# One 2048-column addition per load for the conditioning vectors, in three 8 KB slots, with six weight slots and eight units kept back at the end

## The chip, the cores and the metric

The kernel runs on one core of a Trainium2 chip. The metric is the device time of one launch in microseconds (us). Engines: TensorE (PE) multiplies, its weight loads are PEld; VectorE (DVE) and ScalarE (ACT) work on tiles; GpSimd (POOL) and SyncE (SP) issue transfers. The profile's line numbers are those of the kernel before.

## What is computed

A trunk of two layers on 256 tokens of width 2048, all in float32. Both layers are conditioned by a vector c; the first mixes tokens with a forgetting attention (FoX), the second with a sliding-window attention (SWA), and each is followed by a gated feed-forward block with a short convolution.

```python
c_act = silu(c)
for i in range(2):
    mod = c_act @ ada_w[i] + ada_b[i]            # 2048 x 12288
    sh1, sc1, g1, sh2, sc2, g2 = split(mod, 6)
    h = x * (1 + sc1) + sh1
    y = fox_attention(h, ...) if i == 0 else swa_attention(h, ...)
    x = layer_norm(alpha * x + (1 + g1) * y, ln_mix_g[i], ln_mix_b[i])
    h = x * (1 + sc2) + sh2
    y = conv_ffn(h, ffn_w_up[i], ffn_conv_w[i], ffn_conv_b[i], ffn_w_down[i])
    x = layer_norm(alpha * x + (1 + g2) * y, ln_ffn_g[i], ln_ffn_b[i])
```

## The kernel before

**Weights.** Every product runs through units of 512 KB of weights (256 rows by 512 columns), 728 in all. `stream` (L260) loads a unit into a slot `w` of the pool `wp` (10 slots of 4 KB per partition), ScalarE rounds it to `wh` (L268), and VectorE forms the rest `wl = w - wh` (L279); both lie in the pool `hl`, four pairs. TensorE then makes three products (high by high, high by low, low by high): 24 matmuls of 256 columns, or 12 of 512, per unit. A list `work` holds the units and the steps between them; `settle(2)` (L225) keeps the residuals two units ahead of the matmuls. All loads of `w`, `wa`, `wo` and `ln` are issued by SyncE in program order, each as soon as its slot is free.

**Conditioning vectors.** `mod` isn't computed on TensorE. `ada_vector` (L373) loads `ada_w` in blocks of 128 rows by 1024 columns into slots of the same `wp` pool (tile `wa`) and adds them, each scaled per partition by one column of silu(c), into the accumulator `acc` on VectorE (L395, L397). These operations are pinned, so they keep their program order among the other pinned operations. After each unit `ada_tick` (L469) adds a rate to a debt, and takes one step of `ada_vector` for each whole unit of debt; the rates are written out in the code (1.6 in the FoX projections, 1.3 in its output projection, 0.64 in the first feed-forward block). `ada_need` takes steps until a vector is there. Vectors with an index 2 or 5 are gates: they start from a bias row and are then spread over all partitions, the others are summed by TensorE.

**Opening.** The first two vectors of layer 0 are worked out at once, in five stages of column pairs, from tiles `wo` (L563) of the same pool, partly by additions on VectorE (L574, L576, into `oacc`), partly by products on TensorE (`cps`).

**Other buffers.** `gtile` (L60) gives a tile of 2 KB from the pool `gp` of 30: the FoX partial sums (`part`), the values `v` (L838), `qh`, `ql`, `kh`, `kl`, the gated activations `gT`. `hpad` (`hH`, L480) holds the modulated input in its high and low half, 32 KB per partition.

**Layer norm.** The gains and offsets come as rows, spread over the partitions by `ln_rows` (L659) into four `wp` slots of 1024 columns (tile `ln`), and are used by pinned operations on VectorE (L677, L678, and L1180, L1181 at the end).

**The end.** `x_mm_end` (L298) keeps the last units of the last product back: their matmuls for the first 128 tokens (t0) run at once, those for the other 128 (t1) after all of t0 are done, so that VectorE can finish t0 (`residual` L629, layer norm L1180/L1181, and the output's transfer) meanwhile. Two units are kept in layer 0, four in layer 1.

Of the kernel before, what the change touches and what calls it, by code (L numbers as in the profile page):

```python
# [10 lines left out]
F32 = mybir.dt.float32  # L11
# [30 lines left out]
def hybrid_trunk(ctx: ExitStack, tc: tile.TileContext, a: dict, out: bass.AP):  # L42
# [13 lines left out]
    def wtile(name="w"):  # L56
        return wp.tile([P, 2, WB], F32, tag="w", name=name)

# [201 lines left out]
    def stream(wsrc, row0, col, ks, use):  # L260

        for kc in ks[::2]:
# [3 lines left out]
            h = hl.tile([P, 2, WB], F32R, tag="wh", name="wh")  # L266
            l = hl.tile([P, 2, WB], F32R, tag="wl", name="wl")
# [54 lines left out]

    def x_stationary(wsrc, col, k0, nk, stat, end=0):

        ps = x_banks()
        use = x_mm_end(ps, stat, nk, end) if end else lambda kc, h, l: x_mm(ps, kc, h, l, stat, nk - 1)
        stream(wsrc, k0, col, list(range(nk)), use)
        return ps
# [44 lines left out]
    def ada_vector(l, v):  # L373
# [14 lines left out]
        for k in range(KC):  # L388
            for c in range(0, D, D // 2):
                w = wtile("wa").rearrange("p a f -> p (a f)")  # L390
                pin(nc.sync.dma_start(w, a["ada_w"][l, k * P:(k + 1) * P, v * D + c:v * D + c + D // 2]), False)
                for o in range(0, D // 2, step_):
                    ac, wo = part(c + o, step_), w[:, o:o + step_]
                    if k == 0 and not row:
                        pin(nc.vector.tensor_scalar_mul(ac, wo, cact[:, 0:1]), True)  # L395
                    else:
                        pin(nc.vector.scalar_tensor_tensor(ac, wo, (cactp if row else cact)[:, k:k + 1], ac,  # L397
                                                           op0=ALU.mult, op1=ALU.add), True)
                yield
# [61 lines left out]
    def ada_step():  # L461
        if ada["gen"] is None:
            if not ada_list or ada.get("held"):
                return
            ada["gen"] = ada_vector(*ada_list.pop(0))
        if next(ada["gen"], ada) is ada:
            ada["gen"] = None

    def ada_tick():  # L469
# [65 lines left out]
    def opening(plan, proj, prep):  # L535
# [21 lines left out]
        def sums(s_, c0, CB, acc, ps):  # L557
            QK = 512 // CB
            pe = onpe[s_]
            for kq in range(0, KC, QK):  # L560
                w = wp.tile([P, QK, 2, CB], F32, tag="w", name="wo")
# [647 lines left out]
```

## Time and profile before

| | us |
|---|---|
| median of 3 runs | 2213.51 (2211.17 to 2214.28) |
| profiled execution | 2215.89 |
| its span, first to last instruction | 2214.0 |
| TensorE busy | 2164.3 |
| VectorE busy | 1792.8 |
| ScalarE busy | 1159.6 |
| mean granted TensorE clock | 0.992 |

The busy times are those of the profiled execution, whose span is 1.9 us shorter than its device time. A row of groups names line, engine, operation, the tiles it writes and reads, partitions by elements and count, then busy us and mean ns of one, then the idle time before it and what ended it. In a timeline the first number is the start in us from the span's start, the second the duration, and `x2` two such operations in a row. A row of the DMA issues gives count, KB of one, and the median us from issue to landing.

### The profile page before, as it was taken

What the parts mean: (1) busy time and instruction counts of PE and PEld (TensorE: products, weight loads), DVE (VectorE), ACT (ScalarE), POOL (GpSimd) and SP (SyncE); (2) the same over time, 40 slices, a digit from 0 to 9 for tenths busy, and PEclk for the clock granted to TensorE, in tenths of its full rate; (3) what the DMA queues carried; (4) which work ended last, traced back from release to release, by engine and by line L of the source; (5) the groups of instructions that cost most, each with busy time, mean ns of one, the idle gap of its engine ahead of it and who ended that gap; (6) DMA issues with size and microseconds to landing.
All of it is one profiled execution on the core that took longest, in us unless ns stands there. A gap on an engine that the chain in (4) does not pass through costs nothing. (4 is left out here: it accounts for less than half of the span.)

```text
span 2214.0 us, 38357 instructions
## 1 busy us (share of the span) xinstructions
PE 2164.3 (98%) x14915; PEld 1976.7 (89%) x14915; DVE 1792.8 (81%) x2459; ACT 1159.6 (52%) x1841; POOL 19.0 (1%) x48
## 2 busy tenths in 40 slices
PE   6999999999999999999999999999999999999997
PEld 5999888789999988999987877789999988999986
DVE  6879998989978979799798888789888655666756
ACT  3435656465565543655644677555555533555532
POOL 0000000000000000000000000000000000000000
PEclk9999999999999999999999999999999999999999
DMA  9999998979978989899797676678888566666663
GB/s 334 368 352 366 351 352 298 327 257 323 349 234 300 322 312 385 260 311 322 251 354 290 201 240 206 208 257 295 281 264 270 187 194 195 192 195 195 191 195 108
DMA packets 274246, 602.98 MB, mean 272 GB/s; under 512 B 21062, under 2 KB 29960, under 8 KB 273552
## 3 DMA queue, kind: packets, MB, share of 16 engines
q1 hardware_dynamic: 273008, 595.85, 79.6%
q0 software_dynamic: 1056, 4.69, 0.6%
q8 instruction: 116, 1.90, 0.3%
q14 instruction: 66, 0.54, 0.1%
HBM read 598.37 MB, written 2.10 MB: 271 GB/s over the span
## 5 line engine op out<-in xcount | busy, mean ns | idle before, releaser
L268 ACT CAST wh<-w 128x1024 fp32r<-128x1024 f32 x728 | 765.3, 1053 | 790.0 <-PE ws L75 284.5
L75 PE MATMUL ws<-hH,wh 128*128 128x256 f32 x6656 | 1153.3, 278 | 4.6 <-ACT hH L84 2.1
L279 DVE TENSOR_TENSOR wl<-w,wh 128x1024 fp32r<-128x1024 f32 x728 | 887.6, 1222 | 325.3 <-ACT wh L268 308.5
L75 PEld LDWEIGHTS ws<-hH,wh 128*128 128x128 f32 x6656 | 1012.1, 189 | 9.0 <-ACT hH L84 2.3
L75 PE MATMUL ws<-hH,wl 128*128 128x256 f32 x3328 | 918.6, 277 | 4.3 <-DVE wl L279 4.0
L75 PEld LDWEIGHTS ws<-hH,wl 128*128 128x128 f32 x3328 | 628.5, 189 | 6.0 <-DVE wl L279 5.9
L75 PE MATMUL xs<-wh,gT 128*128 128x512 f32 x1408 | 435.3, 389 | 0.0
L75 PEld LDWEIGHTS xs<-wh,gT 128*128 128x128 f32 x1408 | 264.3, 188 | 54.7
L75 PE MATMUL xs<-wl,gT 128*128 128x512 f32 x704 | 273.9, 389 | 0.0
L75 PE MATMUL xs<-wh,hH 128*128 128x512 f32 x704 | 235.9, 401 | 0.0
L397 DVE SCALAR_TENSOR_TENSOR acc<-wa,cact,acc 128x1024 f32<-128x1024 f32 x180 | 228.4, 1278 | 0.0
L397 DVE SCALAR_TENSOR_TENSOR acc<-wa,cactp,acc 128x1024 f32<-128x1024 f32 x128 | 162.3, 1278 | 0.3 <-DMA acc<-in_ada_b_dram 0.3
L75 PEld LDWEIGHTS xs<-wh,hH 128*128 128x128 f32 x704 | 131.3, 188 | 29.4 <-issue 0.7
L75 PEld LDWEIGHTS xs<-wl,gT 128*128 128x128 f32 x704 | 132.2, 188 | 27.4
L75 PE MATMUL xs<-wl,hH 128*128 128x512 f32 x352 | 138.7, 395 | 2.5 <-DVE wl L279 2.5
L1093 ACT ACTIVATE u<-ws,ccol 128x256 f32<-128x256 f32 x176 | 96.7, 562 | 58.5 <-PE ws L75 43.3
L75 PE MATMUL xs<-wh,oT 128*128 128x512 f32 x384 | 126.2, 397 | 0.8 <-ACT oT L84 0.8
L1094 DVE SCALAR_TENSOR_TENSOR u<-ws,ccol,u 128x255 f32<-128x255 f32 x176 | 82.6, 477 | 14.9 <-ACT u L1093 14.7
L75 PEld LDWEIGHTS xs<-wh,oT 128*128 128x128 f32 x384 | 72.1, 188 | 16.6 <-ACT oT L84 1.2
L1096 DVE SCALAR_TENSOR_TENSOR u<-ws,ccol,u 128x254 f32<-128x254 f32 x176 | 83.1, 477 | 2.2
L75 PEld LDWEIGHTS xs<-wl,hH 128*128 128x128 f32 x352 | 66.5, 189 | 17.5 <-DVE wl L279 4.3
L576 DVE SCALAR_TENSOR_TENSOR oacc<-wo,cact,oacc 128x1024 f32<-128x1024 f32 (+1 forms) x68 | 73.3, 1078 | 8.3 <-DMA wo<-in_ada_w_dram 7.1
(220 smaller groups left out, 1280.4 us busy)
## 6 DMA issues: line engine op xcount, KB each, us to landing
w<-in_ffn_w_up_dram SPq DMA_DIRECT2D x352, 512.0 KB, 4.7
wa<-in_ada_w_dram SPq DMA_DIRECT2D x320, 512.0 KB, 5.6
w<-in_ffn_w_down_dram SPq DMA_DIRECT2D x176, 512.0 KB, 4.9
w<-in_fox_w_in_dram SPq DMA_DIRECT2D x96, 512.0 KB, 6.9
wo<-in_ada_w_dram SPq DMA_DIRECT2D x48, 512.0 KB, 9.0
w<-in_swa_w_in_dram SPq DMA_DIRECT2D x40, 512.0 KB, 4.6
w<-in_fox_w_o_dram SPq DMA_DIRECT2D x32, 512.0 KB, 6.2
w<-in_swa_w_o_dram SPq DMA_DIRECT2D x32, 512.0 KB, 4.8
```

The source lines that it names most:

```text
L75: return nc.tensor.matmul(o, lhsT, rhs, start=start, stop=stop, **kw)
L268: pin(nc.scalar.copy(h, w), False)
L279: pin(nc.vector.tensor_tensor(l, w, f32(h), op=ALU.subtract), behind[0] > 0)
L397: pin(nc.vector.scalar_tensor_tensor(ac, wo, (cactp if row else cact)[:, k:k + 1], ac, op0=ALU.mult, op1=ALU.add), True)
L576: nc.vector.scalar_tensor_tensor(acc, w[:, k], cact[:, kc:kc + 1], acc, op0=ALU.mult, op1=ALU.add)
L1093: nc.scalar.activation(u, pf, AF.Identity, bias=cw(CW, f), scale=cw(2, f))
L1094: nc.vector.scalar_tensor_tensor(u[:, 1:], pf[:, :S - 1], cw(1, f), u[:, 1:], op0=ALU.mult, op1=ALU.add)
L1096: nc.vector.scalar_tensor_tensor(u[:, 2:], pf[:, :S - 2], cw(0, f), u[:, 2:], op0=ALU.mult, op1=ALU.add)
```

## The change

The pool `wp` now has six slots of 4 KB for weights and three of 8 KB (`wide`, tag `wa`). `ada_vector` loads 128 rows by 2048 columns at once and makes one addition of 2048 columns; such a step counts as 2.0 in the debt, so that the same number of columns falls on a unit as before. `gp` has 27 buffers instead of 30. In the opening two of every four `wo` loads share one wide slot, the other two take a weight slot each. `ln_rows` loads gain and offset as one wide tile each instead of two weight slots each. In the last product of layer 1 eight units are kept back instead of four; the high and low tiles of four of the units come from `hpad` instead of `hl` (`spares`). The rate in layer 1's output projection after the need for gate 2 goes from 0.75 to 0.9.

```diff
-    wp = ctx.enter_context(tc.tile_pool(name="wp", bufs=10))
+    wp = ctx.enter_context(tc.tile_pool(name="wp", bufs=6))
-    gp = ctx.enter_context(tc.tile_pool(name="gp", bufs=30))
+    gp = ctx.enter_context(tc.tile_pool(name="gp", bufs=27))
+    def wide(name):
+        return wp.tile([P, D], F32, tag="wa", bufs=3, name=name)
...
-    def stream(wsrc, row0, col, ks, use):
+    def stream(wsrc, row0, col, ks, use, spare={}):
-            h = hl.tile([P, 2, WB], F32R, tag="wh", name="wh")
-            l = hl.tile([P, 2, WB], F32R, tag="wl", name="wl")
+            h, l = spare.get(kc) or (hl.tile([P, 2, WB], F32R, tag=n, name=n) for n in ("wh", "wl"))
...
+    def spares(nk):
+        t = [hpad[:, 56 + i * 2 * WB:56 + (i + 1) * 2 * WB].rearrange("p (a f) -> p a f", a=2) for i in range(8)]
+        return {nk - 16 + 2 * i: (t[2 * i], t[2 * i + 1]) for i in range(4)}
...
         for k in range(KC):
-            for c in range(0, D, D // 2):
-                w = wtile("wa").rearrange("p a f -> p (a f)")
-                pin(nc.sync.dma_start(w, a["ada_w"][l, k * P:(k + 1) * P, v * D + c:v * D + c + D // 2]), False)
-                for o in range(0, D // 2, step_):
-                    ac, wo = part(c + o, step_), w[:, o:o + step_]
-                    if k == 0 and not row:
-                        pin(nc.vector.tensor_scalar_mul(ac, wo, cact[:, 0:1]), True)
-                    else:
-                        pin(nc.vector.scalar_tensor_tensor(ac, wo, (cactp if row else cact)[:, k:k + 1], ac,
-                                                           op0=ALU.mult, op1=ALU.add), True)
-                yield
+            w = wide("wa")
+            pin(nc.sync.dma_start(w, a["ada_w"][l, k * P:(k + 1) * P, v * D:(v + 1) * D]), False)
+            if k == 0 and not row:
+                pin(nc.vector.tensor_scalar_mul(acc, w, cact[:, 0:1]), True)
+            else:
+                pin(nc.vector.scalar_tensor_tensor(acc, w, (cactp if row else cact)[:, k:k + 1], acc,
+                                                   op0=ALU.mult, op1=ALU.add), True)
+            yield 2.0
...
     def ada_tick():
         ada["debt"] += ada["rate"]
         while ada["debt"] >= 1.0:
-            ada["debt"] -= 1.0
-            ada_step()
+            ada["debt"] -= ada_step()
...
-                w = wp.tile([P, QK, 2, CB], F32, tag="w", name="wo")
+                if n % 4 == 0:
+                    two = wide("wo").rearrange("p (b k v f) -> p b k v f", b=2, k=QK, v=2)
+                w = two[:, n % 4] if n % 4 < 2 else wp.tile([P, QK, 2, CB], F32, tag="w", name="wo")
...
     def ln_rows(name, l):
-        gb, bb = [], []
-        for c in range(0, D, D // 2):
-            for b, nm in ((gb, "_g"), (bb, "_b")):
-                w = wtile("ln")
-                nc.sync.dma_start(w.rearrange("p a f -> p (a f)"), a[name + nm][l, c:c + D // 2].partition_broadcast(P))
-                b += [w[:, 0, :], w[:, 1, :]]
-        return gb, bb
+        rows = []
+        for nm in ("_g", "_b"):
+            w = wide("ln")
+            nc.sync.dma_start(w, a[name + nm][l].partition_broadcast(P))
+            rows.append([w[:, c:c + WB] for c in range(0, D, WB)])
+        return rows
...
-        then(lambda: (ada_need(l, 2), ada.update(rate=(1.3, 0.75)[l])))
+        then(lambda: (ada_need(l, 2), ada.update(rate=(1.3, 0.9)[l])))
...
-                ps = x_stationary(w_dn, d * WB, b0 * 4, (b1 - b0) * 4, stat, (2, 4)[l] if si > 0 and d == D // WB - 1 else 0)
+                ps = x_stationary(w_dn, d * WB, b0 * 4, (b1 - b0) * 4, stat, (2, 8)[l] if si > 0 and d == D // WB - 1 else 0)
```

The change moves instructions at several places. On VectorE, in the FoX projections, these are the rows of before from the 69th weight residual on (the number behind a tile's name tells tiles of one name apart):

```order
L279 TENSOR_TENSOR wl_2809<-w_2806,wh_2808 128x1024
L838 TENSOR_TENSOR v_2812<-xs_2500,part_367 128x512
L397 SCALAR_TENSOR_TENSOR acc_2804<-wa_2838,cactp_115,acc_2804 128x1024
L279 TENSOR_TENSOR wl_2844<-w_2841,wh_2843 128x1024
L838 TENSOR_TENSOR v_2847<-xs_2501,part_368 128x512
L397 SCALAR_TENSOR_TENSOR acc_2804<-wa_2873,cactp_115,acc_2804 128x1024
L397 SCALAR_TENSOR_TENSOR acc_2804<-wa_2876,cactp_115,acc_2804 128x1024
L279 TENSOR_TENSOR wl_2882<-w_2879,wh_2881 128x1024
L397 SCALAR_TENSOR_TENSOR acc_2804<-wa_2909,cactp_115,acc_2804 128x1024
L279 TENSOR_TENSOR wl_2917<-w_2914,wh_2916 128x1024
L397 SCALAR_TENSOR_TENSOR acc_2804<-wa_2944,cactp_115,acc_2804 128x1024
L397 SCALAR_TENSOR_TENSOR acc_2804<-wa_2947,cactp_115,acc_2804 128x1024
```

And these are the rows after, from the 73rd residual on:

```order
L281 TENSOR_TENSOR wl_2884<-w_2881,wh_2883 128x1024
L281 TENSOR_TENSOR wl_2928<-w_2925,wh_2927 128x1024
L281 TENSOR_TENSOR wl_2972<-w_2969,wh_2971 128x1024
L857 TENSOR_TENSOR sum_2975<-ws_2696,part_522 128x512
L857 TENSOR_TENSOR sum_3030<-ws_2697,part_523 128x512
L843 TENSOR_TENSOR v_2748<-xs_2448,part_363 128x512
L400 SCALAR_TENSOR_TENSOR acc_2740<-wa_2774,cactp_115,acc_2740 128x2048
L843 TENSOR_TENSOR v_2783<-xs_2449,part_364 128x512
L400 SCALAR_TENSOR_TENSOR acc_2740<-wa_2809,cactp_115,acc_2740 128x2048
L281 TENSOR_TENSOR wl_3027<-w_3024,wh_3026 128x1024
L400 SCALAR_TENSOR_TENSOR acc_2740<-wa_2874,cactp_115,acc_2740 128x2048
L861 SCALAR_TENSOR_TENSOR ql_2978<-sum_2975,qh_2977 128x512
```

Before, the two values `v` stand between the 69th and the 71st residual, and one or two additions after each residual. After, the residuals up to the 75th stand together, and both sums, both `v` and the additions come behind them.

On SyncE's queue, where the layer-norm rows of the first layer's mixer are loaded for use in the feed-forward block, the rows before are:

```order
L391 DMA wa<-in_ada_w_dram 128x1024
L265 DMA w<-in_ffn_w_up_dram 128x2x512
L391 DMA wa<-in_ada_w_dram 128x1024
L664 DMA ln<-in_ln_mix_g_dram 128x1024
L664 DMA ln<-in_ln_mix_b_dram 128x1024
L664 DMA ln<-in_ln_mix_g_dram 128x1024
L664 DMA ln<-in_ln_mix_b_dram 128x1024
L265 DMA w<-in_ffn_w_up_dram 128x2x512 x2
L391 DMA wa<-in_ada_w_dram 128x1024
```

And after, from the last load of `wa` ahead of the rows:

```order
L396 DMA wa<-in_ada_w_dram 128x2048
L268 DMA w<-in_fox_w_o_dram 128x2x512
L669 DMA ln<-in_ln_mix_g_dram 128x2048
L268 DMA w<-in_fox_w_o_dram 128x2x512 x2
L268 DMA w<-in_ffn_w_up_dram 128x2x512 x6
L669 DMA ln<-in_ln_mix_b_dram 128x2048
L268 DMA w<-in_ffn_w_up_dram 128x2x512 x9
L396 DMA wa<-in_ada_w_dram 128x2048
L268 DMA w<-in_ffn_w_up_dram 128x2x512 x2
L396 DMA wa<-in_ada_w_dram 128x2048
L268 DMA w<-in_ffn_w_up_dram 128x2x512 x3
L396 DMA wa<-in_ada_w_dram 128x2048
```

The rows are now two loads of 2048 columns that stand further ahead, among the last weights of the output projection, and no load of `wa` stands between them and the 15 weight loads behind the first; the first `wa` behind the rows is `wa_5148`, the next two are `wa_5256` and `wa_5360`.

At the end, VectorE's rows before, from the third operation of the last layer norm on t0:

```order
L1181 SCALAR_TENSOR_TENSOR x_108<-x_108,rs_23873,ln_23888 128x512 x2
L1180 SCALAR_TENSOR_TENSOR x_108<-x_108,mv_23871,ln_23890 128x512
L632 TENSOR_TENSOR t_23876<-xs_23654,gate_19182 128x512
L1181 SCALAR_TENSOR_TENSOR x_108<-x_108,rs_23873,ln_23892 128x512
L634 TENSOR_TENSOR x_108<-x_108,t_23876 128x512
L638 SCALAR_TENSOR_TENSOR rs_23873<-mv_23871,rs_23873 128x1
L1180 SCALAR_TENSOR_TENSOR x_108<-x_108,mv_23871,ln_23890 128x512
L639 BN_STATS stats_130<-x_108 128x6
L1181 SCALAR_TENSOR_TENSOR x_108<-x_108,rs_23873,ln_23892 128x512
L642 BN_AGGR mv_23881<-stats_130 128x2
L644 TENSOR_SCALAR mv_23881<-mv_23881 128x1
L1180 SCALAR_TENSOR_TENSOR x_108<-x_108,mv_23881,ln_23886 128x512 x2
```

And after:

```order
L650 TENSOR_SCALAR mv_23355<-mv_23355 128x1
L1185 SCALAR_TENSOR_TENSOR x_108<-x_108,mv_23355,ln_23370 128x512 x2
L1186 SCALAR_TENSOR_TENSOR x_108<-x_108,rs_23357,ln_23372 128x512 x2
L1185 SCALAR_TENSOR_TENSOR x_108<-x_108,mv_23355,ln_23370 128x512 x2
L1186 SCALAR_TENSOR_TENSOR x_108<-x_108,rs_23357,ln_23372 128x512 x2
L638 TENSOR_TENSOR t_23360<-xs_23146,gate_18674 128x512
L640 TENSOR_TENSOR x_108<-x_108,t_23360 128x512
L644 SCALAR_TENSOR_TENSOR rs_23357<-mv_23355,rs_23357 128x1
L645 BN_STATS stats_130<-x_108 128x6
L648 BN_AGGR mv_23365<-stats_130 128x2
```

Before, three of t0's last four operations stand between those of t1; after, t0's are all done when t1's first (now L638) comes.

More of the change, by code (lines that the diff above doesn't have):

```diff
@@ L326, in x_stationary @@
         use = x_mm_end(ps, stat, nk, end) if end else lambda kc, h, l: x_mm(ps, kc, h, l, stat, nk - 1)
-        stream(wsrc, k0, col, list(range(nk)), use)
+        stream(wsrc, k0, col, list(range(nk)), use, spares(nk) if end == 8 else {})
         return ps
@@ L463, in ada_step @@
             if not ada_list or ada.get("held"):
-                return
+                return 1.0
             ada["gen"] = ada_vector(*ada_list.pop(0))
-        if next(ada["gen"], ada) is ada:
+        cost = next(ada["gen"], ada)
+        if cost is ada:
             ada["gen"] = None
+        return cost if cost == 2.0 else 1.0
     def ada_tick():
```

2 lines of the change are left out of this document (1 added, 1 removed).

## Prediction

> **What bounds the kernel now.** I read the page's totals first, then the waits of TensorE, then the busy time by stretch.
>
> ```profile
> span 2214.0 us, 38357 instructions
> PE 2164.3 (98%) x14915; PEld 1976.7 (89%) x14915; DVE 1792.8 (81%) x2459; ACT 1159.6 (52%) x1841; POOL 19.0 (1%) x48
> ```
>
> TensorE is busy in 98% of the span, so no edit that leaves its instructions alone can win more than the 49.7 us that are left (2214.0 − 2164.3). VectorE's 81% is an average; the waits say where it is late.
>
> ```profile
> PE cps L75 <- DMA wo<-in_ada_w_dram: 5.7, 3, 4.2
> PE cps L75 <- DVE oacc L576: 5.6, 2, 5.1
> PE xs L75 <- DVE wl L279: 4.2, 4, 1.7
> PE ws L75 <- DVE wl L279: 4.0, 5, 1.4
> ```
>
> The columns are total us, times, longest. TensorE waits 11.3 us for the opening sums (5.7 + 5.6) and only 8.2 us for weight residuals wl from VectorE (4.2 + 4.0), in nine places. The stretches place these:
>
> ```profile
> 0.00:50.00 50.00, 31.96 (x161) 29.81 (x162) 34.29 (x51) 17.96 (x26) 3.67 (x20) 0.94 0.98 329
> 200.00:250.00 50.00, 48.85 (x380) 46.19 (x379) 48.96 (x90) 31.99 (x59) 5.29 (x11) 1.00 0.98 341
> 250.00:300.00 50.00, 48.90 (x373) 45.94 (x372) 46.00 (x60) 29.43 (x76) 0.55 (x1) 1.00 0.99 360
> 300.00:350.00 50.00, 46.40 (x308) 41.27 (x307) 48.66 (x58) 25.71 (x41) 0.00 (x0) 1.00 0.99 358
> 500.00:550.00 50.00, 49.31 (x431) 48.93 (x431) 50.00 (x66) 26.36 (x36) 0.00 (x0) 1.00 0.94 328
> 600.00:1200.00 600.00, 600.00 (x4260) 559.43 (x4259) 519.80 (x608) 308.19 (x460) 0.58 (x1) 1.00 0.90 310
> ```
>
> After the length come the busy times of TensorE, its weight loads, VectorE, ScalarE and GpSimd, then clock, DMA share, GB/s. In 200–350 us (the FoX projections and attention) VectorE is full or nearly so and TensorE loses 5.85 us (1.15 + 1.10 + 3.60). In 500–550 VectorE is at 50.00 of 50 and TensorE loses 0.69. From 600 to 1200 TensorE loses nothing while VectorE is 87% busy: whatever the change saves VectorE there is worth nothing. The DMA share is near 1 in the opening and in 200–350.
>
> **The change part by part.** *(1) Wider additions.* Two 1024-column additions become one of 2048.
>
> ```profile
> L397 DVE SCALAR_TENSOR_TENSOR acc<-wa,cactp,acc 128x1024 f32<-128x1024 f32 x128 | 162.3, 1278 | 0.3 <-DMA acc<-in_ada_b_dram 0.3
> L576 DVE SCALAR_TENSOR_TENSOR oacc<-wo,cact,oacc 128x1024 f32<-128x1024 f32 x42 | 53.8, 1281 | 0.6
> L576 DVE SCALAR_TENSOR_TENSOR oacc<-wo,cact,oacc 128x512 f32<-128x512 f32 x26 | 19.5, 750 | 7.7 <-DMA wo<-in_ada_w_dram 7.1
> 270.45 2.47 DVE L397 SCALAR_TENSOR_TENSOR acc<-wa,cactp,acc 128x1024 f32<-128x1024 f32 x2
> ```
>
> The same operation takes 750 ns for 512 columns and 1281 for 1024, so 531 per 512; 2048 columns are then an estimated 1281 + 2 × 531 = 2343 ns. The pair of today takes 2.47 us: 0.13 saved per pair. Bounds: doubling the step from one addition to the next (2.47 − 1.28 = 1.19) saves nothing, and no row suggests more than 0.2. Over 160 pairs that is 21 us of VectorE, but TensorE waits for wl only in 150–560 us. From the 44th to the 64th weight residual (about 195 to 257 us) the rate of 1.6 halves per unit gives 20 × 0.8 = 16 pairs, 2.1 us at most; TensorE waits there only now and then, so half counts: −1.1 (0 to −2). At 436.9–445 us, where TensorE waits some 2 us for two residuals, the rate leaves VectorE about 1 us less: −1.0 (0 to −1.5).
>
> *(2) What moves on VectorE near 258–305 us.* In the rows of the order, v of part_363 now stands behind both sums, and with it the additions, which are kept in program order; weight residuals stand together ahead. The reason is one `gp` buffer of 27: this v takes the buffer that part_522 leaves when its sum is done. Between the 75th residual (wl_2972) and the 77th (wl_3085) VectorE now has two sums, two v, six wide additions, two ql, two pairs of masked maxima, a reciprocal and two residuals.
>
> ```profile
> 256.31 1.22 DVE L279 TENSOR_TENSOR wl<-w,wh 128x1024 fp32r<-128x1024 f32 x1
> ...
> 285.31 1.28 DVE L852 TENSOR_TENSOR sum<-ws,part 128x512 f32<-128x512 f32 x2
> 286.51 1.22 DVE L279 TENSOR_TENSOR wl<-w,wh 128x1024 fp32r<-128x1024 f32 x1
> 287.64 0.68 DVE L856 SCALAR_TENSOR_TENSOR ql<-sum,qh 128x512 fp32r<-128x512 f32 x1
> 288.24 1.28 DVE L397 SCALAR_TENSOR_TENSOR acc<-wa,cactp,acc 128x1024 f32<-128x1024 f32 x1
> 289.44 0.28 DVE L705 CUSTOM_DVE_ANT_0 pr<-S,mask 128x128 f32<-128x128 f32 x1
> ...
> 289.99 1.22 DVE L279 TENSOR_TENSOR wl<-w,wh 128x1024 fp32r<-128x1024 f32 x1
> ...
> 344.86 1.22 DVE L279 TENSOR_TENSOR wl<-w,wh 128x1024 fp32r<-128x1024 f32 x1
> ...
> 2188.00 0.39 PE L75 MATMUL xs<-wl,gT 128*128 128x512 f32 x1
> 2188.68 0.39 PE L75 MATMUL xs<-wl,gT 128*128 128x512 f32 x1
> ```
>
> From start to start: 1.20 for two sums, 1.13 for a residual, 0.60 for a ql (a v alike), 0.55 for a pair of maxima. So 1.2 + 1.2 + 6 × 2.26 (2.343 less the 0.08 by which neighbours overlap) + 1.2 + 1.1 + 0.07 + 2.27 = 20.6 us, where it is 8.3 in the old order. A unit of weights is 12 matmuls of 512 columns (24 of 256); three take 0.68 us (2188.00 to 2188.68), so a unit takes 2.72. The sum is free once the 72nd unit is multiplied; four units (73 to 76) cover 10.9 us of the 20.6. TensorE also has the attention's matmuls to do, so I take a wait of 6 to 8 us at unit 77. But VectorE has more behind it than it would have today: from the 64th residual (256.31) to the 91st (344.86) pass 88.55 us, of which 82.5 are work by these steps; along the new order the work is 78.0. TensorE loses 4.7 us today in 250–350 (1.10 + 3.60), because VectorE is late. VectorE stands idle some 6 us longer ahead of the sums and has 4.5 us less to do: net +1.5, taken as +1 since it can also make up for some of those 4.7 (−1 to +4).
>
> *(3) Layer-norm rows.* At 490–535 us the rows ln_g and ln_b now hold two of the three wide slots, and the load of wa_5148 waits for the slot of the addition just before it: some 4.4 us of VectorE work lie between that addition and the one that needs the load; for wa_5360 it is about 6.0.
>
> ```profile
> wa<-in_ada_w_dram SPq DMA_DIRECT2D x320, 512.0 KB, 5.6
> w<-in_fox_w_in_dram SPq DMA_DIRECT2D x96, 512.0 KB, 6.9
> wo<-in_ada_w_dram SPq DMA_DIRECT2D x48, 512.0 KB, 9.0
> ```
>
> Half the bytes land in 5.6 us today, so VectorE waits 1 to 3 us, once or twice, and behind the waiting addition on VectorE stand the residuals for which TensorE has hardly a reserve there (50.00 of 50 busy). Behind the load on the sync engine's queue stand weight loads; with six slots of 2.72 us each these have 16 us, against 6.9 to land: no cost. I take +1.5 (0 to +4).
>
> *(4) Opening.* Its prefetch goes from ten slots to about 8.5 loads' worth, and the wide slot comes free only when both halves are used. The DMA share is 0.98 in these 50 us: the queue stays full with eight loads as with ten, so 0 (−1 to +3, a third of the 9.0 us landing, if a gap opens).
>
> *(5) The end.* Eight kept units instead of four: the second row block t1 has 8 × 6 = 48 matmuls left when the first, t0, is complete, 10.9 us instead of 5.45.
>
> ```profile
> 2194.78 0.69 DVE L632 TENSOR_TENSOR t<-xs,gate 128x512 f32<-128x512 f32 x1 [3.13 <-PE xs L75]
> 2196.96 0.26 DVE L642 BATCH_NORM_AGGREGATE mv<-stats 128x2 f32<-128x24 f32 x1
> 2200.63 0.68 DVE L632 TENSOR_TENSOR t<-xs,gate 128x512 f32<-128x512 f32 x1
> 2201.23 0.74 DVE L1181 SCALAR_TENSOR_TENSOR x<-x,rs,ln 128x512 f32<-128x512 f32 x1
> 2201.89 0.68 DVE L634 TENSOR_TENSOR x<-x,t 128x512 f32<-128x512 f32 x1
> 2203.83 0.73 DVE L1181 SCALAR_TENSOR_TENSOR x<-x,rs,ln 128x512 f32<-128x512 f32 x1
> 2204.48 0.26 DVE L642 BATCH_NORM_AGGREGATE mv<-stats 128x2 f32<-128x24 f32 x1
> 2208.82 1.41 DVE L1181 SCALAR_TENSOR_TENSOR x<-x,rs,ln 128x512 f32<-128x512 f32 x2
> ```
>
> For t0 the way from L632 to the aggregate takes 2.18 us (2194.78 to 2196.96); for t1 it takes 3.85 (2200.63 to 2204.48), because three operations of t0 stand between (two are shown, at 2201.23 and 2203.83). With 10.9 us t0 is finished first, and the order has them ahead: −1.67, taken as −1.65 (0 to −2). What follows the aggregate is unchanged. The additional spare buffers lie in hH, unused by then; their loads have at least 4 us in hand.
>
> The second place where the order puts small work together, behind the 96th residual, comes where VectorE is 8 us ahead: nothing. **Sum:** −1.1 + 1 − 1 + 1.5 + 0 − 1.65 = −1.25 us. The profiled execution took 2215.89 us (span 2214.0, 1.9 around it), so it would take 2214.6; the median of the runs, 2213.51, is 2.4 below that execution, so I forecast 2212.3.
>
> **Rivals.** *A, the relief counts in full.* All 8.2 us for wl vanish, since the 0.13 us come off an engine that is full in 200–350 and 500–550, and the cluster is repaid with the 4.5 us that VectorE has less to do. With the end that is −8.2 − 1.65 = −9.9 at most; −7 lies in the middle between that and the 4.4 us named below, 2206.5 on the median. For it: both stretches above. Against it: the waits fall where small operations stand together, not where the additions do.
>
> *B, slower: the cluster isn't repaid.* If the later waits stay where they are, the 6 to 8 us at unit 77 count in full: −1.1 + 7 − 1 + 1.5 − 1.65 = +4.75, so 2218.3. It decides from the point where more than about half of that wait is not made good by unit 91. It has an aggravation that the opening shows:
>
> ```profile
> 43.50 1.67 PE L75 MATMUL cps<-ones,oacc 128*128 128x1 f32 x8 [5.06 <-DVE oacc L576]
> 40.00:50.00 10.00, 6.50 (x31) 6.53 (x32) 8.01 (x11) 2.58 (x4) 0.00 (x0) 0.68 1.05 386
> ```
>
> After an idle stretch of 5.06 us the granted clock averages 0.68 over ten microseconds: 3.2 us of full-speed work lost, as much again as half of the wait. With it B gives +8, 2221.5. The Trainium skill, "TensorE: Matmul & The Clock Gate", in "Part 1: The HAM clock gate (the "warmup" mystery)", says that an idle window of about 3.4 us puts the clock to half until a busy window has passed; the opening agrees. By that rule the wait at unit 77 would be followed by half speed, where today's waits of at most 1.7 us keep the clock at 1.00. I give that a quarter of B's chance rather than all of it, because after the wait VectorE sets the pace, not TensorE.
>
> *C, the opening starves.* Wide slots held by their second half leave the queue empty in 0–56 us: +3 on the sum, 2215.3. Its place is the wait for wo, 5.7 us today. Against it stands the 0.98 share.
>
> *D, the end doesn't move*, because a load for a kept unit is late: +1.65, so 2214; the four microseconds in hand speak against it.
>
> **How the numbers follow.** About 0.2% (4.4 us) is what a measurement of this kernel can tell from no change. My forecast has 0.36 (of which 0.02 is beyond −4.4 us and 0.02 beyond +4.4, by the tails of the unknown terms), C 0.05 and D 0.03, both within; A has 0.34, of which 0.32 is beyond −4.4; B has 0.22, all beyond +4.4. So within 0.2% has 0.32 + 0.05 + 0.03 + 0.02 = 0.42, faster 0.34, slower 0.24. The predicted time is the forecast's, 2212.3. The forecast's own range is −4 to +4 about its median. The range that holds 8 in 10 reaches down to −8.0 (A without its last part), 2205.5, and up to +6 (B without the clock), 2219.5.
>
> **What would show each step.** (1) the wide addition at 2.3 to 2.4 us in the groups. (2) In the timeline a wait of TensorE for wl of more than 4 us at 290–305 us, and a clock below 1.00 in the stretch after it (B) or not; then fewer waits in 305–345. (3) VectorE waiting on a DMA for wa in 500–530. (4) the waits for wo and oacc near 5.7 and 5.6. (5) t1's L632 to its aggregate at 2.2 us with nothing of t0 between. I am wrong if TensorE's loss in 250–350 moves by more than 4 us from today's 4.7, or if a stretch beyond 560 loses anything.

## The result and the profile after

The changed kernel takes 2234.07 us (median of 5, 2225.91 to 2235.32), before 2213.28 (2211.17 to 2214.28): slower by 21 us by the medians, where 1 us faster was forecast. The five executions are unevenly spread, with a mean of 2231.98; the ratio, which weighs all of them, is 1.0084 (95% interval 1.0073 to 1.0095), so 19 us. The changed kernel was not timed again beside the experiments: "less than after" and "slower than after" below are differences of medians, and the means would put every such kernel 1 to 3 us higher against after. The profiled execution took 2234.07, its span 2231.3, 17.3 us longer than before. A few executions were disturbed: two took twice the time (one of b_tail, and one of a_rate, of which only the times are used), and one of b_tail5 took 2237.45 us at a clock of 0.945; without it the mean of that run lies 1.7 us below before's.

The totals of the profile after, as the page gives them:

```profile
span 2231.3 us, 37689 instructions
PE 2173.8 (97%) x14915; PEld 1984.4 (89%) x14915; DVE 1772.4 (79%) x2299; ACT 1165.4 (52%) x1843; POOL 19.1 (1%) x48
```

VectorE did lose work: 20.4 us (1792.8 to 1772.4), in 160 operations fewer. TensorE has the same 14915 matmuls and is busy 9.5 us longer with them (2173.8 against 2164.3). So, as an account of time and not yet of causes, more than half of the 17.3 us is the same work at a lower clock, and 7.8 us are new idle time. What TensorE waits for most, in total us, times and longest:

```profile
PE cps L78 <- DVE oacc L582: 6.3, 2, 5.8
PE cps L78 <- DMA wo<-in_ada_w_dram: 5.7, 3, 4.2
PE ws L78 <- DVE wl L281: 4.9, 7, 2.1
PE sm L189 <- DVE posf L186: 4.3, 1, 4.3
PE ws L78 <- ACT wh L270: 4.0, 3, 3.2
PE S L78 <- ACT A L874: 3.7, 2, 2.0
```

The opening's two waits are as before (12.0 us in all, 11.3 before). New are `posf` and `A`, and the waits for `wh` grew from 1.3 us in all to 4.0: none of these is a weight residual. The stretches that answer to those of before:

```profile
200.00:250.00 50.00, 41.99 (x322) 41.25 (x321) 40.15 (x73) 30.69 (x55) 5.33 (x11) 0.90 0.77 273
250.00:300.00 50.00, 45.90 (x288) 41.19 (x287) 38.69 (x36) 26.48 (x61) 0.55 (x1) 0.94 0.91 335
300.00:350.00 50.00, 49.22 (x341) 45.13 (x340) 49.93 (x58) 25.84 (x51) 0.00 (x0) 0.99 0.97 351
500.00:550.00 50.00, 46.77 (x385) 45.91 (x384) 45.00 (x55) 25.99 (x34) 0.00 (x0) 0.97 0.77 247
600.00:1200.00 600.00, 600.00 (x4354) 563.11 (x4353) 511.81 (x549) 313.25 (x470) 0.58 (x1) 1.00 0.89 310
```

In 200–250 us TensorE's busy time fell from 48.85 to 41.99, and the clock from 1.00 to 0.90. VectorE, at 48.96 before, is at 40.15: it isn't the full engine there any more; it waits too. From 600 to 1200 TensorE loses nothing, as before.

To place the loss exactly I count the units by their products with `wl` in each trace and compare the start of the same unit in two executions. The table gives what each stretch of units lost (+) against before's profile, in us; the columns behind after are kernels told of below. The stretches add up to the whole (17.3 us for after).

| units | about us (before) | after | b_gp27 | a_gp29w5 | a_posearly | a_comb3 |
|---|---|---|---|---|---|---|
| 1–49, opening and projections | 0–202 | −1.6 | −0.8 | +3.9 | −2.0 | +3.1 |
| 49–53, positions | 202–214 | +6.0 | +0.4 | +0.8 | 0.0 | +1.2 |
| 53–69, first attention heads | 214–271 | +4.0 | +0.3 | +2.4 | +4.4 | −0.1 |
| 69–93, sums, `v`, gate | 271–356 | +9.3 | +13.0 | +3.4 | +7.0 | +2.5 |
| 93–137 | 356–502 | −0.9 | 0.0 | −0.9 | −1.0 | −1.4 |
| 137–149, layer-norm rows | 502–536 | +4.4 | 0.0 | +4.5 | +1.4 | −1.3 |
| 149–481 | 536–1524 | −1.9 | −0.1 | −2.0 | −2.0 | −1.7 |
| behind 481, the end | 1524–2214 | −2.0 | 0.0 | −2.0 | −2.0 | −2.0 |

Each column is one execution. Kernels whose edits lie elsewhere still differ from after by some us at a place: units 1–49 lie between −2.0 and +2.5 in a_posearly, a_sin, a_ln4 and a_possin, units 69–93 lose 7.0 to 7.1 in a_sin, a_possin and a_posearly, and units 137–149 lose 1.4 to 2.6 in these three. Smaller differences than these say nothing here. The 1.9 us won at units 149–481 lie almost all at units 437–445 (1373 to 1408 us).

**The sums and `v` (69–93).** VectorE after, in the place that the prediction worked out:

```profile
288.86 1.23 DVE L281 TENSOR_TENSOR wl<-w,wh 128x1024 fp32r<-128x1024 f32 x1 [1.49 <-ACT wh L270]
290.00 1.29 DVE L857 TENSOR_TENSOR sum<-ws,part 128x512 f32<-128x512 f32 x2
291.21 0.68 DVE L843 TENSOR_TENSOR v<-xs,part 128x512 f32<-128x512 f32 x1
291.81 2.34 DVE L400 SCALAR_TENSOR_TENSOR acc<-wa,cactp,acc 128x2048 f32<-128x2048 f32 x1
294.07 0.68 DVE L843 TENSOR_TENSOR v<-xs,part 128x512 f32<-128x512 f32 x1
...
309.49 1.22 DVE L281 TENSOR_TENSOR wl<-w,wh 128x1024 fp32r<-128x1024 f32 x1
```

From the first sum (290.00) to the end of the 77th residual (309.49 + 1.22) pass 20.7 us; 20.6 were worked out. By unit 77 TensorE is 7.2 us further behind than at unit 69. But it doesn't stop at the 77th unit. It stops earlier, at two matmuls of the attention:

```profile
292.58 0.33 PE L78 MATMUL S<-Bm,A 128*128 128x128 f32 x1 [2.01 <-ACT A L874]
295.44 0.48 PE L78 MATMUL S<-Bm,A 128*128 128x128 f32 x1 [1.68 <-ACT A L874]
```

`A` is a `gp` tile as well, written by ScalarE:

```profile
291.93 0.60 ACT L874 ACTIVATE A<-A,sel 128x256 fp32r<-128x256 f32 x1 [0.39 <-DVE v L843]
294.79 1.09 ACT L874 ACTIVATE A<-A,sel 128x256 fp32r<-128x256 f32 x2 [2.26 <-DVE v L843]
```

Each starts as a `v` ends, which the profile gives as what it waits for: it takes a buffer of the partial sum that this `v` has read, and the second stands behind the wide addition at 291.81. The clock by five microseconds there, and at the gate's spreading at 364 us, where TensorE waits 1.54 us for `ah`:

```profile
285.00:290.00 5.00, 5.00 (x47) 5.00 (x46) 2.37 (x2) 2.11 (x2) 0.00 (x0) 1.00 1.01 344
290.00:295.00 5.00, 1.75 (x14) 1.35 (x12) 5.00 (x7) 1.85 (x3) 0.00 (x0) 0.88 0.47 148
295.00:300.00 5.00, 4.56 (x21) 4.56 (x22) 5.00 (x3) 2.00 (x4) 0.00 (x0) 0.50 0.95 316
300.00:305.00 5.00, 5.00 (x43) 5.00 (x42) 5.00 (x6) 2.08 (x4) 0.00 (x0) 0.94 0.99 341
...
365.00:370.00 5.00, 4.77 (x18) 4.08 (x18) 2.66 (x8) 3.83 (x9) 0.00 (x0) 0.55 1.04 413
370.00:375.00 5.00, 5.00 (x25) 4.35 (x25) 2.11 (x9) 4.70 (x14) 0.00 (x0) 0.77 0.87 338
```

These clocks are 5 × (0.12 + 0.50 + 0.06) = 3.4 us of full speed at the first place and 5 × (0.45 + 0.23) = 3.4 us at the second. What they cost is told by a_sin (an edit at the positions, below), which has the same two waits for `A` (2.01 and 1.68 us) and the same wait of 1.54 us for `ah`, but another clock behind them:

```profile
290.00:295.00 5.00, 1.77 (x12) 1.57 (x12) 5.00 (x5) 2.20 (x4) 0.00 (x0) 0.97 0.65 175
295.00:300.00 5.00, 5.00 (x33) 5.00 (x32) 5.00 (x5) 1.23 (x3) 0.00 (x0) 0.69 0.98 378
...
365.00:370.00 5.00, 4.46 (x32) 3.83 (x30) 3.16 (x12) 5.00 (x16) 0.00 (x0) 1.00 1.03 409
```

At the first place a_sin has 5 × (0.03 + 0.31) = 1.7 us of lost clock instead of 3.4, and units 69–81 lose 7.25 us in both: VectorE's chain up to the 77th residual sets the pace there, and the half clock costs nothing more (a_sin's TensorE waits 1.14 us for `pr` there, behind VectorE, after's 0.27). Units 81–89 make 2.9 us good in both. At the second place, units 89–93, a_sin loses no clock and 2.7 us, after 5.0: there the clock costs 2.3. (a_ln4, with a half clock there too, loses 5.0; a_posearly and a_possin, without it, 2.7.) `ah` stands on ScalarE behind a cast of weights that itself waits 1.62 us for TensorE.

**The positions (49–53).** VectorE, TensorE, and the time from issue to landing of the positions' load, first after, then before:

```profile
211.18 0.21 DVE L186 CAST posf<-posr 2x128 f32<-2x128 int32 x1 [3.43 <-DMA posr<-in_positions_dram]
```

```profile
211.45 0.22 PE L189 MATMUL sm<-ident,posf 2*128 2x2 f32 x1 [4.30 <-DVE posf L186]
```

```profile
DMA to landing us min/median/max: 7.6/7.6/7.6
```

```profile
DMA to landing us min/median/max: 4.4/4.4/4.4
```

The order of this cast and this small transpose hardly moved. The load of 1 KB took 4.4 us to land before and the cast came just behind it, without a wait; now it takes 7.6, among loads of 1 MB, and both engines stand still behind it in program order. That the larger loads make it late is likely and not shown: in two kernels with the same 1 MB loads and fewer weight slots it took 5.4 and 4.9 us.

**The first heads (53–69).** ScalarE before, where the cosine stands ahead of the first exponential (L709), and after:

```profile
223.92 0.22 ACT L210 ACTIVATE cost<-nturn 128x16 f32<-128x16 f32 x1 [0.80 <-DVE nturn L207]
...
225.11 1.28 ACT L709 ACT_TABLE_LOAD   x1
226.41 0.40 ACT L709 ACTIVATE pr<-pr,nm 128x128 f32<-128x128 f32 x1
```

```profile
229.32 1.28 ACT L714 ACT_TABLE_LOAD   x1 [1.43 <-DVE nm L710]
...
231.12 1.28 ACT L213 ACT_TABLE_LOAD   x1
232.41 0.22 ACT L213 ACTIVATE cost<-nturn 128x16 f32<-128x16 f32 x1
...
233.60 1.28 ACT L714 ACT_TABLE_LOAD   x1
...
235.40 1.03 ACT L270 CAST wh<-w 128x1024 fp32r<-128x1024 f32 x1
```

The cosine now stands between two exponentials (L714), which gives two more table loads, and the cast of the next weights comes behind them: TensorE waits 3.2 us for `wh`.

**The layer-norm rows (137–149)** and **the end**:

```profile
DVE acc L400 <- DMA wa<-in_ada_w_dram: 3.7, 2, 2.5
```

```profile
2219.53 0.69 DVE L638 TENSOR_TENSOR t<-xs,gate 128x512 f32<-128x512 f32 x1 [2.95 <-PE xs L78]
...
2221.71 0.26 DVE L648 BATCH_NORM_AGGREGATE mv<-stats 128x2 f32<-128x24 f32 x1
```

VectorE waits 3.7 us in two waits for a wide load, as worked out; t1's way takes 2.18 us (2221.71 − 2219.53).

### The profile page after: what moved, and what is told of

It reads as the page before. It is cut to its first block, busy times and chain, and to the rows that moved or that the text cites. A ratio compares the mean times of both kernels' runs of the same rounds, so it can differ in the third digit from the quotient of the medians.

```text
span 2231.3 us, 37689 instructions
## 1 busy us (share of the span) xinstructions
PE 2173.8 (97%) x14915; PEld 1984.4 (89%) x14915; DVE 1772.4 (79%) x2299; ACT 1165.4 (52%) x1843; POOL 19.1 (1%) x48
## 4 chain that ended last, share of the span: by engine, by line
PE 83%; DVE 7%; DMA 5%; issue 3%; ACT 2%; SPq 0%; POOL 0%; DVEq 0%; ACTq 0%; POOLq 0%
PE ws L78 45%; PE xs L78 34%; DVE acc L400 2%; DMA w<-in_fox_w_in_dram 2%; DVE wl L281 2%; DMA wo<-in_ada_w_dram 1%; DMA wa<-in_ada_w_dram 1%; ACT wh L270 1%; PE S L78 1%; PE o L78 1%; PE T L741 1%; PE cps L78 1%; PE sm L500 1%; PE sm L442 0%; DVE oacc L582 0%
## 5 line engine op out<-in xcount | busy, mean ns | idle before, releaser
L78 PE MATMUL xs<-wh,gT 128*128 128x512 f32 x1376 | 425.7, 389 | 0.0
L78 PEld LDWEIGHTS xs<-wh,gT 128*128 128x128 f32 x1376 | 258.3, 188 | 53.5
L78 PE MATMUL xs<-wl,gT 128*128 128x512 f32 x688 | 267.7, 389 | 0.0
L400 DVE SCALAR_TENSOR_TENSOR acc<-wa,cact,acc 128x2048 f32<-128x2048 f32 x90 | 210.9, 2343 | 0.2 <-issue 0.2
L400 DVE SCALAR_TENSOR_TENSOR acc<-wa,cactp,acc 128x2048 f32<-128x2048 f32 x64 | 150.0, 2344 | 3.7 <-DMA wa<-in_ada_w_dram 3.7
```

Of the source, the lines that this page charges most:

```text
L78: return nc.tensor.matmul(o, lhsT, rhs, start=start, stop=stop, **kw)
L400: pin(nc.vector.scalar_tensor_tensor(acc, w, (cactp if row else cact)[:, k:k + 1], acc, op0=ALU.mult, op1=ALU.add), True)
```

## The experiments

The theory after the result: each part of the loss has its own place and its own small cause, and the largest is the missing `gp` buffers. Its rival: the wide loads and their few slots make everything late.

**b_gp27.** One number of the kernel before:

```diff
-    gp = ctx.enter_context(tc.tile_pool(name="gp", bufs=30))
+    gp = ctx.enter_context(tc.tile_pool(name="gp", bufs=27))
```

> Kernel of before with 27 instead of 30 buffers in gp, nothing else. Order theory (a missing gp buffer lets the values v and all additions behind them wait for a sum, so that residuals come late): 5 to 12 us slower than before, the loss between the 69th and the 93rd unit, with a clock below 1.00 behind it. Load theory (the 1 MB loads and their three slots are what is late): no change, within 1 us of before, because loads and slots are those of before.

Measured: 2226.39 us against 2214.76 for before beside it, ratio 1.0057 (1.0042 to 1.0072). All of it lies at units 69–93 (+13.0 in the table). VectorE waits for the first sum, with `v` and the additions behind it, and TensorE stops at the same matmul:

```profile
281.52 1.37 DVE L852 TENSOR_TENSOR sum<-ws,part 128x512 f32<-128x512 f32 x2 [5.28 <-PE ws L75]
```

```profile
284.18 0.33 PE L75 MATMUL S<-Bm,A 128*128 128x128 f32 x1 [2.02 <-ACT A L869]
```

```profile
285.00:290.00 5.00, 4.39 (x25) 4.19 (x24) 5.00 (x6) 3.06 (x5) 0.00 (x0) 0.66 0.75 203
```

So three buffers fewer cost 12 us without any wide load. The order theory holds here in place, price and clock, though what comes late first is `A` and not a residual; the load theory falls for this place.

**a_gp29w5.** The kernel after with two buffers given back, paid with a weight slot:

```diff
-    wp = ctx.enter_context(tc.tile_pool(name="wp", bufs=6))
+    wp = ctx.enter_context(tc.tile_pool(name="wp", bufs=5))
...
-    gp = ctx.enter_context(tc.tile_pool(name="gp", bufs=27))
+    gp = ctx.enter_context(tc.tile_pool(name="gp", bufs=29))
```

> Kernel of after with 29 buffers in gp and, to make room, five weight slots instead of six. Order theory: 7 to 12 us faster than after (7 at the 69th to 81st unit, up to 5 more at the 91st to 93rd). Load theory: no faster, rather 1 to 4 us slower, since a weight slot is missing.

Measured: 2224.76, 9.3 less than after; ratio to before 1.0051 (1.0036 to 1.0066). Units 69–93 lose 3.4 instead of 9.3, and no matmul waits for `A`; the same five microseconds that had a clock of 0.50:

```profile
295.00:300.00 5.00, 5.00 (x46) 5.00 (x45) 4.19 (x10) 3.25 (x9) 0.00 (x0) 1.00 1.02 410
```

The missing slot seems to cost up to 5.5 us in the opening and the first projections (+3.9 against −1.6; the two other kernels with five slots have +2.9 and +3.1 there, but a_possin with six has +2.5). The wait for the positions went too, since their load landed in 5.4 us here (0.7 us of waiting are left); that wasn't meant.

**a_gp30w4.** The same with `bufs=4` for weights and `bufs=30` for `gp`.

> Kernel of after with 30 buffers in gp and four weight slots instead of six, which is the memory of before. Order theory: the 13 us that 27 buffers cost between the 69th and the 93rd unit are gone, so 9 to 13 us faster than after if four slots cost 0 to 4. Rival (weight slots matter more than gp): no faster, or slower, with waits for w loads spread over all stages.

Measured: 2249.40, 15 us slower than after: a miss. By unit 49 it is 24.5 us behind before, and only 8.1 us are added from there to unit 93 (19.3 in after). With all 30 buffers units 69–93 still lose 4.0, so a part of the loss there has another cause, which no run here separates. Weight slots matter in the opening, where wide `wo` tiles and weights share the queue, and not only a little; this was no way to test `gp`.

**b_tail** and **b_tail5.** The kernel before with `spares`, the `spare` argument and `(2, 8)[l]` of the diff, the second time in five rounds.

> Kernel of before with the end of after alone (eight units kept back, spare tiles in hpad). Theory: 1.7 us faster than before (1.5 to 2.0), all of it behind the last unit. Rival (late loads for the kept units): no change.

> The kernel of before with the end of after alone, once more and in five rounds, to see whether it is faster than before beyond doubt. Theory: 1.7 to 2.1 us faster than before, ratio 0.9991, interval below 1. Rival: the difference lies in the spread of the runs, interval across 1.

Measured: 2212.01 against 2214.76, ratio 0.9988 (0.9979 to 0.9998); then 2212.32 against 2213.63, ratio 1.0003 (0.9984 to 1.0023). The end in the trace is 2.0 us shorter than before's both in this kernel and in after, so the mechanism is as forecast. As a time the gain is seen once and lost in the spread once, by the execution of 2237.45 us. Its medians are the only ones here below those of both kernels.

**a_ln4.** `ln_rows` of before in the kernel after, four weight slots instead of two wide ones.

> Kernel of after whose layer-norm rows are loaded as before, in four tiles of 1024 columns in weight slots. Slot theory (the rows hold two of the three wide slots, so additions wait for their load): 4 us faster than after, at the 139th to 145th unit. Rival (VectorE has too much work there whatever the slots): within 1 us of after. Second rival: four of six weight slots held by the rows starve the weights, 4 us or more slower.

Measured: 2238.31, 4.2 slower than after. Units 125–149 lose 2.5 us instead of 4.7, which is no more than the scatter (1.6 to 2.7 in a_posearly, a_sin and a_possin), but 4.1 us are lost anew at the next layer norm (units 325 to 421). VectorE no longer waits for a load of `wa`, as the slot theory has it, and four of six weight slots starve the weights elsewhere, as its second rival has it: at 1000–1320 us ScalarE waits 20.1 us for loads of weights, in after for none.

**a_narrow.** Wide loads, two additions of 1024 for each:

```diff
-                pin(nc.vector.scalar_tensor_tensor(acc, w, (cactp if row else cact)[:, k:k + 1], acc,
-                                                   op0=ALU.mult, op1=ALU.add), True)
+            for c in (slice(0, D // 2), slice(D // 2, D)):
...
+                    pin(nc.vector.scalar_tensor_tensor(acc[:, c], w[:, c], (cactp if row else cact)[:, k:k + 1], acc[:, c],
+                                                       op0=ALU.mult, op1=ALU.add), True)
```

> Kernel of after with the same loads of 2048 columns, but each added in two operations of 1024 columns. Forecast's step (the wider addition saves 0.13 us per pair, nearly all of it where nothing waits for it): 0 to 3 us slower than after. Rival A (relief of VectorE counts in full where TensorE waits): 5 us or more slower than after.

Measured: 2238.64, 4.6 slower than after (6.5 by the means). In the changed kernel the wider addition is worth more than the forecast's 2.1 and about what rival A asked, 5; in the trace it lies at units 77–93 (5.0 us lost, 2.1 in after), 141–149 (4.9, 4.0 in after) and 149–481 (0.2 lost, 1.9 won in after).

**a_sin.** Sine and cosine in one tile and one operation:

```diff
...
-        nc.scalar.activation(sint, ang, AF.Sin)
-        nc.scalar.activation(cost, nturn, AF.Sin)
+        nc.scalar.activation(trig, an, AF.Sin)
```

> Kernel of after with sine and cosine of the positions in one ScalarE operation instead of two. Table theory (at the 53rd to 61st unit the two are parted by an exponential, which gives four table loads of 1.28 us ahead of a cast of weights): 3 to 5 us faster than after, TensorE's wait for wh (3.2 us) gone. Rival (the wait for the positions' load, 4.3 us, and the clock behind it are the whole loss there): within 1 us of after.

Measured: 2232.66, 1.4 less than after. TensorE's wait of 3.2 us for `wh` is still there: ScalarE first waits 3.97 us for VectorE, then the one operation still stands between two exponentials, with its own table load and one back. A miss.

**a_possin.** a_sin, and two more `yield` behind the positions' load.

> Kernel of after with both: one operation for sine and cosine, and the use of the loaded positions two steps later than their load. If both waits at the 49th to 61st unit are the cause of the 10 us lost there: 7 to 10 us faster than after, all lost time at these units gone, and clock 1.00 in 200 to 250 us. Rival (VectorE is late there anyway, through the wide additions): no more than 4 us faster.

Measured: 2226.26, 7.8 less than after. The 11.1 us lost at units 49–61 (−1.6 to +9.5 behind) become 3.1 (+2.5 to +5.6), not nothing as was expected, and the clock is 1.00 in 200–250. The intervals of the two ratios overlap (1.0046 to 1.0080, after from 1.0073). Here the sine came behind both exponentials of a head.

**a_posearly.** Only the load moves:

```diff
+    posr = cst.tile([NT, P], I32, name="posr")
+    nc.gpsimd.dma_start(posr, a["positions"].rearrange("b (t p) -> (b t) p", p=P))
...
-        posr = tp.tile([NT, P], I32, tag="t", name="posr")
-        nc.gpsimd.dma_start(posr, a["positions"].rearrange("b (t p) -> (b t) p", p=P))
```

> Kernel of after whose positions are loaded at the start into a tile of their own; the order of all else stays as in after but for three small rows. Landing theory (the positions' 1 KB land 7.6 us after their issue behind the 1 MB loads, instead of 4.4, and VectorE and TensorE stand in order behind the operation that needs them): TensorE's wait of 4.3 us is gone, and with the clock behind it 5 to 9 us less time than after. Rival (the late exponentials and casts on ScalarE at 229 to 236 us are what costs): the time is only made up for until there, within 2 us of after.

Measured: 2226.16, 7.9 less than after. Units 49–53 lose nothing any more, 6.0 in after. The profiled execution, at 2221.53 the fastest of the four, is also better at other places with the same order (units 69–93 lose 7.0 instead of 9.3, 137–149 1.4 instead of 4.4); a_sin and a_possin are so too, so this needn't be the edit.

**a_rotfirst.** a_posearly with the rotary tables first, so that sine and cosine are together ahead of all exponentials:

```diff
-        later([forget(), columns(), rotary(), scaled()])
+        later([rotary(), forget(), columns(), scaled()])
```

> Kernel of after with the positions loaded at the start, and the preparation of the rotary tables taken as the first of the four background tasks instead of the third, so that sine and cosine stand together ahead of the first exponential on ScalarE. Table theory (the wait of TensorE for wh of 3.2 us at the 53rd to 57th unit and the half clock behind it come from the sine between two exponentials): 5 us faster than the kernel with the early positions alone, 12 to 14 us faster than after, 2220 to 2222. Rival (ScalarE waits for VectorE there, 4 us, whatever the tables): within 2 us of the kernel with the early positions alone, 2226.

Measured: 2229.29 (2223.22 to 2232.74), no faster than a_posearly: a miss as a time. At the place itself the theory holds in part: TensorE's wait for `wh` is gone, and units 53–57 lose 2.2 us, 5.0 in a_posearly. The profiled execution, at a clock of 0.989, lost more elsewhere: 5.1 us up to unit 49, and one wait of 5.3 us for `A` at the sums.

**a_rate.** No conditioning steps while the rows hold the slots:

```diff
-            then(lambda: ada.update(rate=(0.64, 0.4)[l]))
+            then(lambda si=si: ada.update(rate=0.0 if l == 0 and si == 0 else (0.64, 0.4)[l]))
             for b in range(b0, b1):
+                if l == 0 and b == 1:
+                    then(lambda: ada.update(rate=0.77))
```

> Kernel of after in which no step of the conditioning vectors is taken in the first 16 units of the first feed-forward block, and the rate is 0.77 instead of 0.64 in the 80 units behind them, so that no load of wa waits for a slot while the layer-norm rows hold two of three. Slot theory: 4 us faster than after, at the 137th to 149th unit, and VectorE waits on no load of wa there. Rival (VectorE has too much work there or, with 0.77, behind it): within 1 us of after, or slower with new waits for wl in 545 to 800 us.

Measured: 2225.80 to 2230.25 us, ratio to before 1.0064 (1.0049 to 1.0078), 1.0084 for after: some 4 to 5 us faster, though the intervals touch. The place is shown by a_comb2.

**a_comb2** joins a_gp29w5, a_posearly and a_rate; **a_comb3** adds a_rotfirst's order.

> Kernel of after with the three cures together: 29 buffers in gp (five weight slots), the positions loaded at the start, no conditioning steps in the first 16 units of the first feed-forward block. If the causes are separate and add up: 7 for gp, 5 to 9 for the positions, 4 for the rows, so 16 to 20 us faster than after, 2214 to 2218, with what five slots cost (some 4 us at the 37th unit) included. Rival (the causes share their loss, one wait merely takes the place of another): no more than 12 us faster than after.

> All four cures together: 29 buffers in gp with five weight slots, early positions, rotary tables first, no conditioning steps in the first 16 units of the first feed-forward block. If the table theory holds, 4 to 6 us less than the three cures together (2219.66): 2214 to 2216, level with before. If the opening's and the five slots' loss is all that remains there, the excess over before is at the 21st to 37th unit. Rival: 2219 to 2220 again.

Measured: a_comb2 2219.66, 14.4 less than after (11.2 by the means), between the 16 to 20 expected and the rival's 12; units 137–149, where a_gp29w5 loses 4.5 us and a_posearly 1.4, now gain 1.3, and VectorE waits on no load of `wa` there. The causes are separate in place but seem to share some of their price (a_gp29w5 alone had already lost the positions' wait). a_comb3: 2216.81 against 2214.39, ratio 1.0011 (1.0002 to 1.0021), a little above the 2214 to 2216 expected. Its totals:

```profile
span 2214.2 us, 37661 instructions
PE 2161.7 (98%) x14915; PEld 1971.7 (89%) x14915; DVE 1773.4 (80%) x2299; ACT 1163.0 (53%) x1841; POOL 18.9 (1%) x48
```

The span is before's 2214.0 to within 0.2, TensorE's busy time is 2.6 us below before's (2164.3), and VectorE has 19.4 us less to do. With four small edits nearly all of the loss is gone: 2.4 us are left between the medians, nothing between the spans of the two profiles. On balance what VectorE saves buys nothing here. What stands against the gain is +3.1 up to unit 49, where the sixth weight slot is missing, and 2.5 at the sums.

## Why the prediction was wrong

It forecast −1.25 us for the profiled execution; +17.3 came. By its steps:

1. *Wider additions.* The size is right: 2343 ns were estimated, and the row reads so:

```profile
L400 DVE SCALAR_TENSOR_TENSOR acc<-wa,cact,acc 128x2048 f32<-128x2048 f32 x90 | 210.9, 2343 | 0.2 <-issue 0.2
```

   The second part of its worth came where it was put (−1.0 forecast at 437–445 us, −0.9 at units 93–137). The whole, −2.1, was too small for the changed kernel: a_narrow makes it 4.6, and its trace has 2.1 behind unit 149, where none was forecast.

2. *The cluster.* **This is the step that failed.** The order was read rightly, the 20.6 us were 20.7, and the 6 to 8 us of loss by unit 77 came as 7.2. That they would come as a wait for `wl` was wrong: TensorE waits for `A`, a tile of the same starved pool, and the step asked only who waits for `wl`. The conclusion "net +1.5, taken as +1 (−1 to +4)" was wrong by more. It set the 4.5 us that VectorE has less to do against TensorE's loss, but TensorE can win back only what it used to lose by waiting for VectorE: its waits for `wl` behind 260 us fell from 3.3 us (before, up to 370) to 0.7 (after, up to 380), and units 81–89 made 2.9 us good, where a net of +1 asks for 6. And it had nothing at the gate's spreading, units 89–93, which lost 5.0 us in after and 2.7 in a_sin. So units 69–93 lost 9.3 (7.0 in a_sin), and b_gp27 shows that 27 buffers alone cost 11.6.

   This was rival B, which had 0.22, apart from the tile that is waited for. For the cluster it had 7 us, and 3.2 of clock in the case to which a quarter of its chance was given, "because after the wait VectorE sets the pace". At the sums that reason holds, as a_sin shows; at the gate's spreading it does not, where the clock costs 2.3. That 7 and 3.2 together are near the 9.3 is partly luck, since the clock is charged at another place. Its +8 in all falls short of +17.3 by what is named under 6.

3. *Layer-norm rows.* +1.5 (0 to +4) forecast, +4.4 in the profiled execution, by the mechanism named. The two waits sum to 3.7 us, as worked out; that TensorE would pay all of it and a stretch at 0.97 was not. With the same rows a_posearly, a_sin and a_possin lose 1.4, 2.0 and 2.6 there, so the range was right and the row at most under-sized.

4. *Opening.* 0 forecast, −1.6 up to unit 49, which is within the scatter (b_tail5, whose opening is before's, has −2.8). The share of the DMA engines was a sound reason with six slots; with four it wasn't (+24.5), and with five perhaps not (+2.9 to +3.9).

5. *The end.* −1.65 forecast, −2.0 measured.

6. *Not in the prediction at all:* the positions' load and the cosine, +10 at units 49–69, the same size as the cluster. The places of the order that the prediction looked at were those of weight residuals, additions and the end; two small unpinned tasks, each under 0.3 us on its engine, were passed over. The load hardly moved in the order; that what runs beside it makes it late is likely, not shown. a_posearly shows the first of the two; the second is shown in part (a_possin, a_rotfirst).

The Trainium skill, "TensorE: Matmul & The Clock Gate", in "Part 1: The HAM clock gate (the "warmup" mystery)", has the half clock follow an idle window of about 3.4 us. The trace agrees on the half, 0.50 in 295–300 us, but not on the length: idle stretches of 2.01 and 1.68 us with a few matmuls between them sufficed, and one of 1.54 at 364. Nor does the length of one wait decide: the same 1.54 us in a_sin, and before's 1.71 at 437 and 1.44 at 326, left the clock at 1.00:

```profile
435.00:440.00 5.00, 3.29 (x15) 2.42 (x14) 5.00 (x5) 1.04 (x1) 0.00 (x0) 1.00 0.85 243
440.00:445.00 5.00, 4.98 (x22) 3.70 (x22) 5.00 (x6) 1.99 (x2) 0.00 (x0) 1.00 0.96 359
```

The measurement decides: in this kernel a wait of some 1.5 us is followed by 3.4 us of lost clock in one execution and by none in another.

What stays open: when the clock falls behind such a wait, which may be a good part of the spread of the changed kernel, 2225.91 us at a clock of 0.993 to 2235.32 at 0.988; what the 4.0 us are that units 69–93 lose with all 30 buffers; and why a_rotfirst loses 5.1 us up to unit 49.

## What to carry to other kernels

When a change takes buffers from a pool, list every tile that comes from it and follow each to the engine that reads it first, not only the stream that is usually late. Where engines run in program order, a small load that came just in time can become a wait when the transfers beside it change: look in the profile for operations that come within a fraction of a microsecond of their landing. What another engine saves gives TensorE back no more than TensorE waits for that engine today: book the saving against those waits, and not against a new loss. And price a new wait of TensorE with a possible stretch of half clock behind it, which here cost between nothing and 2.3 us for a wait of 1.54.

## What the runs showed of the hardware

The same 1 KB load, issued from GpSimd's queue, landed in 4.4 to 5.1 us in the four profiles with 512 KB conditioning loads around it (before, b_gp27, b_tail, b_tail5), in 4.9 to 7.6 us in the seven with 1 MB loads, and in 3.1 or 3.3 us where it was issued at the start. One operation of 2048 columns takes 2343 ns, where two of 1024 in a row take 2.47 us. And table loads of ScalarE take 1.28 us each: an operation of 0.22 us between two of another table takes 2.8 us with its load and the load back.
